# Two trunk layers on one core: hi and lo of an activation in one 512-column matmul, seven PSUM banks in one rotation, the queries' norm in the softmax

## The chip, the cores and the metric

One of the eight cores of a Trainium2 chip. The time is the device time of one execution in microseconds (us). PE is TensorE's matmul stream, PEld its weight loads, DVE VectorE, ACT ScalarE, POOL GpSimd, SP SyncE, which issues nearly all the DMAs.

## The reference, cut to what matters

256 tokens, 1024 channels, two layers, all float32. Only products with a weight matrix matter here:

```python
for l in range(DEPTH):                                  # DEPTH = 2
    u = rms_norm(h, norm_mix_g[l])
    p = u @ w_in[l]                                     # 1024 -> 10240: q, k, v, g_ret, c_in, gates
    y_a = (silu(g_ret) * o) @ w_ret_out                 # 2048 -> 1024, o: group-normed chunk retention
    y_b = c @ w_conv_out + b_conv_out                   # c: 31-tap conv, layer norm, silu
    h = h + (g_a * y_a + g_b * y_b) @ w_mix_out
    q = rms_norm(h, norm_xattn_g[l]) @ w_xq             # 4 heads of 256
    k, v = split(rms_norm(mem, norm_mem_g[l]) @ w_xkv)  # 256 memory tokens
    s = einsum("bshd,bmhd->bhsm", q, k) * 256 ** -0.5
    h = h + (softmax(s) @ v) @ w_xo
    val, gate = split(rms_norm(h, norm_ffn_g[l]) @ w_up)      # 1024 -> 2 * 2816
    h = h + (silu(causal_dwconv3(gate)) * val) @ w_down       # 2816 -> 1024
```

## The kernel before

Activations lie with the channel on the partitions: a block is 128 x 8 x 256 (8 channel tiles of 128, 256 tokens). Float32 precision is kept with two halves in a faster matmul format: `x = hi + lo`, and a product is the sum of three, `wh*uh + wh*ul + wl*uh`. So every weight and every activation has a hi tile and a lo tile.

`prepare` (lines 126 to 134) makes a weight *unit* (128 x 1024, eight channel tiles by 128 outputs): ACT copies the raw weights into `whi` (L131), DVE subtracts for `wlo` (L132). There are four places for units (UNITS), so unit u+4 can be made only when PE is done with unit u. `split` (L163, L164) does the same for an activation.

`feat` (L172 to L174) multiplies one unit with a block: per channel tile three matmuls of 256 columns, `wh` by `uh`, `wh` by `ul`, `wl` by `uh`, each with its own weight load, all summed into one half of a PSUM bank (a bank is 128 x 512). `both` (L274) is the same with two units taken in turn. `tok` (L185) is for products with the token on the partitions (v, g and the memory's v): there the weights move, 512 columns wide.

`run` goes through a list of steps, most of them two units wide: 40 for the in-projection (16 of them `tok`), then `w_ret_out`, `w_conv_out`, one chunk of the memory's keys (`mem_k`), `w_mix_out`, three more `mem_k`, the queries (`w_xq`) with attention between them, `w_xo`, `w_up`, `w_down`. The work between the steps (evacuation of banks, norms, retention, softmax) is recorded in program order, marked urgent in places, and put in order for each engine by a list scheduler that simulates the program.

PSUM has four banks in a rotation for these products (`mm`), three for attention (`att`) and one for the norms' sums (`nrm`). `residual` (L336) adds a bank to the residual stream `h`, squares it for the next norm, and, where a gain is given (`gained`), makes the hi and lo of `h * gain` at once (`early`), so that the next product can begin before its norm is known; its result is scaled afterwards (`scaled`). The queries don't do that: `normalise` builds normed hi and lo blocks under `mem_k` steps 1 to 3, and the softmax uses the constant 1/16.

Of the kernel before, what the change touches and what calls it, by code (L numbers as in the profile page):

```python
# [13 lines left out]
P = 128  # L14
# [30 lines left out]
BLOCKS = 10  # L45
# [6 lines left out]
def by_token(x):  # L52
    return x.rearrange("p k n -> p (k n)").rearrange("p (t d) -> p t d", t=2)

# [9 lines left out]
class Trunk:  # L64
# [19 lines left out]

    def block(self, dt=F32, tag="blk", bufs=BLOCKS):
        return self.bp.tile([P, KT, N], dt, name=self.nm(tag), tag=tag, bufs=bufs)
# [7 lines left out]
    def bank(self, tag="mm", bufs=4):  # L94
        return self.pp.tile([P, 2, N], F32, name=self.nm(tag), tag=tag, bufs=bufs)

# [78 lines left out]

    def tok(self, outs, ws, u, half):
# [13 lines left out]
    def flat_banks(self):  # L190
        return [self.bank().rearrange("p t n -> p (t n)") for _ in range(2)]
# [121 lines left out]
    @urgent  # L313
    def normalise(self, gname, layer, keep=False):
        r = self.spread(self.pending)
        if keep:
            self.rstd = self.small([N], "rstd", bufs=1)
            self.nc.scalar.activation(self.rstd, r, AF.Copy)
        return self.normed(self.h, r, gname, layer)

    def normed(self, h, rstd, gname, layer):
        nc = self.nc
        uh, ul = self.block(F32R), self.block(F32R)
        for j in range(KT // 2):
# [5 lines left out]
            self.split(u, uh[:, 2 * j:2 * j + 2, :], ul[:, 2 * j:2 * j + 2, :])  # L330
        return uh, ul
# [101 lines left out]

    def memory(self, layer):

        nc = self.nc
        m = self.block()
        nc.sync.dma_start(m, self.io["mem"])
# [6 lines left out]
        self.xk = self.block(F32R), self.block(F32R)  # L445
        self.xv = self.block(F32R), self.block(F32R)

    def mem_k(self, layer, c, midway=None):
        def fn(*w):
            ps, pr = self.bank(), slice(2 * c, 2 * c + 2)  # L450
            self.each(ps, w, self.mem, midway)
            self.split(ps, self.xk[0][:, pr, :], self.xk[1][:, pr, :])
        self.step(fn, *self.pair("w_xkv", layer, c))

    def mem_v(self, layer, c):

        def fn(*w):
            if c % 2 == 0:
# [9 lines left out]
    def mixer(self, layer):  # L468
# [5 lines left out]
        def alloc_conv():  # L474
            X["c"], X["cc"] = self.block(), self.block()

        def start():
            X["u"] = self.normalise("norm_mix_g", L, keep=True)
# [59 lines left out]
        def scores(h):  # L538
            ps = self.bank("att", 3).rearrange("p t n -> p (t n)")
# [9 lines left out]
        def attend(h):  # L549
            s, v = X["s", h], X["v", h]  # L550
            for n in range(2):
                ps = self.bank("att", 3).rearrange("p t n -> p (t n)")
# [18 lines left out]
        def gate(h):  # L571
            pt = [self.bank("att", 3) for _ in range(2)]
# [4 lines left out]
            hi, lo = X["y"]  # L577
            b, r = h // 2, (h % 2) * 4
            for f in range(4):
                src, gain = pt[f // 2][:, f % 2, :], self.par("ret_gn_g", L, 4 * h + f)  # L580
                yh, yl = hi[b][:, r + f, :], lo[b][:, r + f, :]
# [23 lines left out]
        def alloc_y():  # L605
            X["y"] = ([self.block(F32R), self.block(F32R)], [self.block(F32R), self.block(F32R)])
# [24 lines left out]
        def alloc_gates():  # L631
            X["gt"] = (self.block(), self.block())
# [16 lines left out]
        def alloc_m():  # L649
            X["m"] = self.block()  # L650
        self.step(alloc_m)
        for f in range(KT):
            def fn(*w, f=f):
                if f % 2 == 0:
                    X["ps"] = self.bank()
                hi, lo = X["y"]
                out = X["ps"][:, f % 2, :]
                for b in range(2):
                    self.feat(out, w[b], (hi[b], lo[b]), first=b == 0, last=b == 1)
                if f % 2:  # L660
                    pr = slice(f - 1, f + 1)
                    nc.vector.tensor_tensor(X["m"][:, pr, :], X["ps"], X["gt"][0][:, pr, :], op=ALU.mult)
            self.step(fn, *self.pair("w_ret_out", L, f))
            if f == MEM_AT:
# [11 lines left out]
        def conv_norm(self):  # L676
# [7 lines left out]
            r = self.spread(self.rsqrt(pair_sum(sq), LN_EPS))  # L684
            nc.vector.tensor_tensor(cc, cc, bc(r), op=ALU.mult)
            for k in range(KT):
                nc.scalar.activation(cc[:, k, :], cc[:, k, :], AF.Silu,
                                     scale=self.par("conv_ln_g", L, k),
                                     bias=self.par("conv_ln_b", L, k))
            X["z"] = self.block(F32R), self.block(F32R)  # L690
            self.split(cc, *X["z"])

        def alloc_mm():
            X["mm"] = self.block(F32R), self.block(F32R)
        self.step(alloc_mm)
        for j in range(4):
            def fn(*w, j=j):
                ps = self.bank()
                for f in range(2):
                    self.feat(ps[:, f, :], w[f], X["z"])  # L700
# [6 lines left out]
                m = X["m"][:, pr, :]  # L707
# [5 lines left out]
        self.begin()  # L713
# [300 lines left out]
```

## Time and profile before

| | |
|---|---|
| time, median of 3 runs | 1297.48 us (1297.29 to 1298.04) |
| profiled execution | 1297.52 us, its span 1295.7 us |
| PE busy | 1278.4 us, 99% of the span |
| PE's weight loads busy | 1225.2 us, 95% |
| DVE busy | 972.8 us, 75% |
| ACT busy | 857.7 us, 66% |
| TensorE's granted clock, mean | 0.997 of full speed |

The span runs from the first to the last instruction; the time of an execution has 1.8 us more. Busy time of PE says that matmuls were under way, not how fast they follow each other: a 256-column matmul is listed with some 283 ns, but several are in flight at once. How fast they follow is read from starts, or from a run of them and its count.

### The profile page before, as it was taken

Reading aid. Unit: us, or ns where it says so; the run is one execution under the profiler, and the core shown is the slowest. Engines: PE = TensorE matmul, PEld = TensorE weight load, DVE = VectorE, ACT = ScalarE, POOL = GpSimd, SP = SyncE. Lnnn points to the kernel's source line nnn. Section 1 sums busy time; section 2 is a strip of 40 time slices with the busy share of each in tenths; the row PEclk is TensorE's granted clock in tenths of the full one; section 3 lists DMA queues with packets and bytes.
Section 4 is the critical chain, followed back from the end, with each engine's and each line's share of the span. In section 5 each row is a group of like instructions: output and inputs, shape, how many; then the busy total and the mean of one; then the engine's idle time right before and its main releaser. Section 6 shows DMA issues by size and latency. Waiting matters only on the chain.

```text
span 1295.7 us, 23296 instructions
## 1 busy us (share of the span) xinstructions
PE 1278.4 (99%) x9632; PEld 1225.2 (95%) x9632; DVE 972.8 (75%) x1283; ACT 857.7 (66%) x1365; POOL 27.9 (2%) x31
## 2 busy tenths in 40 slices
PE   7999999999999999999999999999999999999997
PEld 7998888999999999999999888899999989999997
DVE  8989998767676688665677999985686766876653
ACT  6899999664445557664469899986454554666542
POOL 0000000000000000000000010000000000000000
PEclk9999999999999999999999999999999999999998
DMA  8554444555554445544555444444654544455450
GB/s 306 208 180 163 163 158 169 193 187 194 178 190 137 157 168 192 190 163 181 189 190 183 170 158 172 163 165 162 228 190 172 176 147 163 169 189 189 156 178 33
DMA packets 33082, 227.32 MB, mean 175 GB/s; under 512 B 3920, under 2 KB 4176, under 8 KB 6736
## 3 DMA queue, kind: packets, MB, share of 16 engines
q1 hardware_dynamic: 32688, 225.32, 49.4%
q8 instruction: 75, 1.23, 0.4%
q10 hardware_dynamic: 288, 0.52, 0.1%
q14 instruction: 31, 0.25, 0.1%
HBM read 224.78 MB, written 1.05 MB: 174 GB/s over the span
## 4 chain that ended last, share of the span: by engine, by line
PE 84%; issue 14%; DMA 0%; DVE 0%; ACT 0%; SPq 0%; POOLq 0%; POOL 0%; DVEq 0%
PE mm L172 20%; PE mm L173 20%; PE mm L174 20%; PE mm L185 17%; PE mm L274 3%; PE att L553 1%; PE att L745 1%; PE att L746 1%; PE att L744 1%; PE att L575 1%; PE att L542 1%; PE att L555 1%; PE nrm L211 0%; DMA raw<-in_w_in_dram 0%; PE nrm L203 0%
## 5 line engine op out<-in xcount | busy, mean ns | idle before, releaser
L172 PE MATMUL mm<-blk,whi 128*128 128x256 f32 x2624 | 745.4, 285 | 0.0
L173 PE MATMUL mm<-blk,whi 128*128 128x256 f32 x2624 | 742.3, 283 | 0.0
L174 PE MATMUL mm<-blk,wlo 128*128 128x256 f32 x2624 | 742.2, 283 | 0.0
L131 ACT ACTIVATE whi<-raw 128x1024 fp32r<-128x1024 f32 (+1 forms) x424 | 443.2, 1050 | 346.4 <-PE mm L173 270.7
L132 DVE TENSOR_TENSOR wlo<-raw,whi 128x1024 fp32r<-128x1024 f32 (+1 forms) x424 | 511.0, 1211 | 193.8 <-ACT whi L131 191.9
L172 PEld LDWEIGHTS mm<-blk,whi 128*128 128x128 f32 x2624 | 502.8, 192 | 2.6 <-issue 1.7
L173 PEld LDWEIGHTS mm<-blk,whi 128*128 128x128 f32 x2624 | 503.0, 192 | 2.3 <-issue 2.2
L174 PEld LDWEIGHTS mm<-blk,wlo 128*128 128x128 f32 x2624 | 502.9, 192 | 0.3 <-issue 0.2
L185 PE MATMUL mm<-whi,blk 128*128 128x512 f32 x640 | 201.9, 391 | 0.0
L499 ACT ACTIVATE prod<-blk,params 128x255 f32<-128x255 f32 (+14 forms) x480 | 197.2, 487 | 3.8 <-DVE blk L502 3.8
L502 DVE TENSOR_TENSOR blk<-blk,prod 128x1020 f32<-128x1020 f32 (+14 forms) x120 | 138.2, 1151 | 7.9 <-ACT prod L499 6.8
L185 PEld LDWEIGHTS mm<-whi,blk 128*128 128x128 f32 x640 | 119.6, 188 | 25.1 <-issue 1.2
L185 PE MATMUL mm<-wlo,blk 128*128 128x512 f32 x320 | 128.2, 401 | 0.0
L185 PEld LDWEIGHTS mm<-wlo,blk 128*128 128x128 f32 x320 | 60.1, 188 | 12.8 <-issue 0.7
L163 ACT ACTIVATE blk<-t 128x512 fp32r<-128x512 f32 (+1 forms) x71 | 42.5, 614 | 16.1 <-DVE t L261 12.4
L164 DVE TENSOR_TENSOR blk<-t,blk 128x512 fp32r<-128x512 f32 (+1 forms) x71 | 47.0, 676 | 2.6 <-ACT blk L163 2.6
L274 PE MATMUL mm<-blk,whi 128*128 128x256 f32 x192 | 39.7, 295 | 7.9 <-ACT whi L131 7.9
L274 PEld LDWEIGHTS mm<-blk,whi 128*128 128x128 f32 x192 | 32.5, 201 | 7.9 <-ACT whi L131 7.9
L848 DVE SCALAR_TENSOR_TENSOR t<-t,params,t 128x255 f32<-128x255 f32 (+1 forms) x88 | 38.2, 478 | 0.0
L336 DVE TENSOR_TENSOR h<-mm,h 128x512 f32<-128x512 f32 (+1 forms) x26 | 16.9, 650 | 20.9 <-PE mm L174 16.0
L274 PE MATMUL mm<-blk,wlo 128*128 128x256 f32 x96 | 28.3, 295 | 1.1 <-DVE wlo L132 1.1
L218 POOL TENSOR_TENSOR rs_r<-rs_m,mhalf 128x2 f32<-128x2 f32 x11 | 8.5, 777 | 888.5 <-DVE rs_m L217 888.5
(133 smaller groups left out, 742.4 us busy)
## 6 DMA issues: line engine op xcount, KB each, us to landing
raw<-in_w_in_dram SPq DMA_DIRECT2D x79, 1024.0 KB, 4.9
raw<-in_w_up_dram SPq DMA_DIRECT2D x44, 1024.0 KB, 4.9
raw<-in_w_ret_out_dram SPq DMA_DIRECT2D x16, 1024.0 KB, 4.9
raw<-in_w_xkv_dram SPq DMA_DIRECT2D x16, 1024.0 KB, 4.9
raw<-in_w_down_dram SPq DMA_DIRECT2D x16, 1024.0 KB, 5.0
raw<-in_w_conv_out_dram SPq DMA_DIRECT2D x8, 1024.0 KB, 5.8
raw<-in_w_mix_out_dram SPq DMA_DIRECT2D x8, 1024.0 KB, 4.8
raw<-in_w_xq_dram SPq DMA_DIRECT2D x8, 1024.0 KB, 4.8
```

The lines of the kernel that those rows point to most:

```text
L131: nc.scalar.activation(hi[:, :n], raw, AF.Copy)
L132: nc.vector.tensor_tensor(lo[:, :n], raw, hi[:, :n].bitcast(F32), op=ALU.subtract)
L163: self.nc.scalar.activation(hi, src, AF.Copy)
L164: self.nc.vector.tensor_tensor(lo, src, hi.bitcast(F32), op=ALU.subtract)
L172: self.nc.tensor.matmul(out, wh[:, k, :], uh[:, k0 + k, :], start=a, stop=False)
L173: self.nc.tensor.matmul(out, wh[:, k, :], ul[:, k0 + k, :], start=False, stop=False)
L174: self.nc.tensor.matmul(out, wl[:, k, :], uh[:, k0 + k, :], start=False, stop=b)
L185: mm = lambda a, b, p, q: self.nc.tensor.matmul(out, a[:, k, ts], b[:, j, :], start=p, stop=q)
L274: mm = lambda x, y, a, b: self.nc.tensor.matmul(out, x[:, k, :], y[:, k, :], start=a, stop=b, skip_group_check=True)
L499: nc.scalar.activation(t[:, i, :m], X["c"][:, k, :m], AF.Copy, scale=self.par("conv_dw_w", L, k * TAPS + TAPS - 1 - s))
L502: nc.vector.tensor_tensor(cc, cc, t[:, :, :m], op=ALU.add)
L848: nc.vector.scalar_tensor_tensor(g[:, f, s:], x[:, f, :N - s], wt(k, 2 - s), g[:, f, s:], op0=ALU.mult, op1=ALU.add)
```

## The change

1. Outside the in-projection (and the four chunks that run ahead of a norm), `feat` and `both` give way to `wide`: hi and lo of an activation lie side by side in one tile (`halved`, 128 x 8 x 2 x 256), and one matmul moves both, 512 columns, past `wh` into a whole PSUM bank; `wl` by `uh` follows with 256 columns into the bank's first half. The three partial products now lie in two halves of a bank.
2. The halves have to be added: `add_up` copies the second half to SBUF on ACT (L213) and adds the first on DVE (L214). `residual` adds all four halves to `h` on DVE (L380), with no copy.
3. The seven banks other than the norms' are one rotation; a product of two units takes two banks, not one.
4. The queries are made from `early`, hi and lo of `h * gain`, and the token's factor goes into the softmax's scale and maximum (`scale`, L778); the normed blocks for the queries are gone, two of the `mem_k` steps stand later, between the queries.
5. Smaller: `gained` takes hi by a scaled copy on ACT and lo by one DVE operation; blocks come in pairs; the memory's input lies in one of the four places for raw weights and is fetched two steps before its use; the conv norm's end goes in four pieces; in the FFN the gate's copy out of PSUM is gone.

```diff
+    def halved(self):
+        return Split(self.bp.tile([P, KT, 2, N], F32R, name=self.nm("blk"), tag="blk", bufs=BLOCKS))
...
-    def bank(self, tag="mm", bufs=4):
+    def bank(self, tag="mm", bufs=BANKS):
...
+    def wide(self, ps, w, u, first=True, last=True):
+        kt = w[0].shape[1]
+        for k in range(kt):
+            self.nc.tensor.matmul(ps, w[0][:, k, :], u.tile[:, k], start=first and k == 0, stop=False)
+            self.nc.tensor.matmul(ps[:, 0, :], w[1][:, k, :], u[0][:, k, :], start=False, stop=last and k == kt - 1)
+
+    def wides(self, w, u):
+        pair = self.banks()
+        for f in range(2):
+            self.wide(pair[f], w[f], u)
+        return pair
+
+    def add_up(self, pair):
+        t = self.temp()
+        for f, ps in enumerate(pair):
+            self.nc.scalar.activation(t[:, f, :], ps[:, 1, :], AF.Copy)
+            self.nc.vector.tensor_tensor(t[:, f, :], ps[:, 0, :], t[:, f, :], op=ALU.add)
+        return t
...
     def gained(self, k, n):
...
-            t, pr = self.temp(), slice(k, k + n)
-            for i in range(n):
-                nc.vector.tensor_scalar(t[:, i, :], self.h[:, k + i, :], self.par(*self.gain, k + i), None,
-                                        op0=ALU.mult)
-            self.split(t[:, :n, :], self.early[0][:, pr, :], self.early[1][:, pr, :])
+            for i in range(k, k + n):
+                hi, lo = (x[:, i, :] for x in self.early)
+                g = self.par(*self.gain, i)
+                nc.scalar.activation(hi, self.h[:, i, :], AF.Copy, scale=g)
+                nc.vector.scalar_tensor_tensor(lo, self.h[:, i, :], g, hi.bitcast(F32), op0=ALU.mult,
+                                               op1=ALU.subtract)
...
     @urgent
-    def residual(self, ps, k, n=2):
+    def residual(self, banks, k):
+        n = len(banks)
         h = self.h[:, k:k + n, :]
-        self.nc.vector.tensor_tensor(h, ps, h, op=ALU.add)
+        for f, ps in enumerate(banks):
+            for i in range(2):
+                self.nc.vector.tensor_tensor(h[:, f, :], ps[:, i, :], h[:, f, :], op=ALU.add)
         self.ssq_add(k, n, h)
         self.gained(k, n)
...
+    def fetch_memory(self):
+
+        raw = self.wp.tile([P, 2048], F32, name=self.nm("raw"), tag="raw", bufs=RAWS)
+        self.nc.sync.dma_start(raw, self.io["mem"])
...
-        def start():
-            X["u"] = self.normalise("norm_xattn_g", L)
-            X["o"] = self.block(F32R), self.block(F32R)
-        self.mem_k(L, 1, self.scale_of_h)
-        self.mem_k(L, 2, start)
-        self.mem_k(L, 3)
+        @urgent
+        def scale(self):
+
+            X["r"] = self.small([2], "xr", bufs=1)
+            nc.vector.tensor_scalar(X["r"], self.rms_scale()[1], 0.0625, None, op0=ALU.mult)
+        self.mem_k(L, 1)
...
-            nc.vector.tensor_scalar(nb, mx, -0.0625, None, op0=ALU.mult)
+            nc.vector.scalar_tensor_tensor(nb, mx, -1.0, X["r"], op0=ALU.mult, op1=ALU.mult)
...
-                nc.scalar.activation(p[:, t, :], ps[:, t, :], AF.Exp, scale=0.0625,
+                nc.scalar.activation(p[:, t, :], ps[:, t, :], AF.Exp, scale=X["r"][:, t:t + 1],
```

Three places show how the instructions move. First PE, at the end of one unit and the start of the next in `w_up` of layer 0 (L172 to L174 are `feat`'s three matmuls, L200 and L201 `wide`'s two; behind the arrow what is written and read, then partitions by columns). Before:

```order
L173 MATMUL mm_817_5464<-blk_787_5312,whi_805_5391 128x256
L174 MATMUL mm_817_5464<-blk_786_5311,wlo_806_5392 128x256
L172 MATMUL mm_817_5464<-blk_786_5311,whi_807_5395 128x256
L173 MATMUL mm_817_5464<-blk_787_5312,whi_807_5395 128x256
L173 MATMUL mm_825_5533<-blk_787_5312,whi_813_5456 128x256
L174 MATMUL mm_817_5464<-blk_786_5311,wlo_808_5396 128x256
```

Of the change:

```order
L200 MATMUL mm_881_5452<-blk_800_4973,whi_868_5393 128x512
L201 MATMUL mm_881_5452<-blk_800_4973,wlo_869_5394 128x256
L200 MATMUL mm_889_5508<-blk_800_4973,whi_876_5443 128x512
L201 MATMUL mm_889_5508<-blk_800_4973,wlo_877_5444 128x256
L200 MATMUL mm_889_5508<-blk_800_4973,whi_876_5443 128x512
```

Three matmuls of 256 columns have become one of 512 and one of 256, and each unit fills a bank of its own.

Second DVE, at the residual adds of `w_mix_out` in layer 0 (L132 and L151 are the weights' lo, L336 and L380 the adds to `h`, L231 and L272 the norm's sum of squares, L304 the lo of `early`). Before:

```order
L132 TENSOR_TENSOR wlo_578_3866<-raw_576_3863,whi_577_3865 128x1024
L336 TENSOR_TENSOR h_77<-mm_574_3811,h_77 128x512
L132 TENSOR_TENSOR wlo_580_3870<-raw_576_3863,whi_579_3869 128x1024
L132 TENSOR_TENSOR wlo_586_3930<-raw_584_3927,whi_585_3929 128x1024
L336 TENSOR_TENSOR h_77<-mm_581_3873,h_77 128x512
L132 TENSOR_TENSOR wlo_588_3934<-raw_584_3927,whi_587_3933 128x1024
L231 TENSOR_TENSOR t2_583_3925<-t2_575_3861,t2_582_3923 128x512
```

Of the change:

```order
L380 TENSOR_TENSOR h_77<-mm_584_3704,h_77 128x256
L151 TENSOR_TENSOR wlo_590_3753<-raw_588_3750,whi_589_3752 128x1024
L380 TENSOR_TENSOR h_77<-mm_585_3705,h_77 128x256
L151 TENSOR_TENSOR wlo_592_3757<-raw_588_3750,whi_591_3756 128x1024
L380 TENSOR_TENSOR h_77<-mm_593_3760,h_77 128x256
L304 SCALAR_TENSOR_TENSOR blk_575_3649<-h_77,params_76,blk_575_3649 128x256
L151 TENSOR_TENSOR wlo_599_3809<-raw_597_3806,whi_598_3808 128x1024
L304 SCALAR_TENSOR_TENSOR blk_575_3649<-h_77,params_76,blk_575_3649 128x256
L272 TENSOR_TENSOR t2_587_3744<-t2_578_3688,t2_586_3742 128x512
L304 SCALAR_TENSOR_TENSOR blk_575_3649<-h_77,params_76,blk_575_3649 128x256
```

Between the weights' subtractions stand now single 256-column adds of four banks and the lo of `early`, where one 512-column add stood.

Third PE, inside `w_mix_out` of layer 0, where the last pieces of its input come late. Before, two banks are worked on in turn, the first two steps' first units:

```order
L174 MATMUL mm_574_3811<-blk_538_3488,wlo_565_3743 128x256
L172 MATMUL mm_574_3811<-blk_538_3488,whi_564_3742 128x256
L172 MATMUL mm_581_3873<-blk_538_3488,whi_570_3803 128x256
L173 MATMUL mm_581_3873<-blk_539_3489,whi_570_3803 128x256
L174 MATMUL mm_581_3873<-blk_538_3488,wlo_571_3804 128x256
```

Of the change, four banks (576, 577, 584, 585) and with them all four units are worked on in turn, and the next two units follow at once:

```order
L200 MATMUL mm_584_3704<-blk_530_3377,whi_571_3641 128x512
L201 MATMUL mm_584_3704<-blk_530_3377,wlo_572_3642 128x256
L200 MATMUL mm_585_3705<-blk_530_3377,whi_573_3645 128x512
L201 MATMUL mm_585_3705<-blk_530_3377,wlo_574_3646 128x256
L200 MATMUL mm_585_3705<-blk_530_3377,whi_573_3645 128x512
L201 MATMUL mm_585_3705<-blk_530_3377,wlo_574_3646 128x256
L200 MATMUL mm_593_3760<-blk_530_3377,whi_580_3696 128x512
L200 MATMUL mm_594_3761<-blk_530_3377,whi_582_3700 128x512
L201 MATMUL mm_593_3760<-blk_530_3377,wlo_581_3697 128x256
```

So the four places for units come free within a short stretch there, and their successors are wanted right behind it.

## Rows read from the trace of the kernel before

**Rows 1.** The page: busy time, clock in 40 slices, chain, one kind of DMA issue.

```profile
span 1295.7 us, 23296 instructions
PE 1278.4 (99%) x9632; PEld 1225.2 (95%) x9632; DVE 972.8 (75%) x1283; ACT 857.7 (66%) x1365; POOL 27.9 (2%) x31
...
PEclk9999999999999999999999999999999999999998
...
PE 84%; issue 14%; DMA 0%; DVE 0%; ACT 0%; SPq 0%; POOLq 0%; POOL 0%; DVEq 0%
...
raw<-in_w_ret_out_dram SPq DMA_DIRECT2D x16, 1024.0 KB, 4.9
```

**Rows 2.** The waits: who waited for whom, us in total, times, longest.

```profile
PE mm L274 <- ACT whi L131: 7.9, 1, 7.9
PE mm L274 <- DVE wlo L132: 1.1, 2, 0.7
PE nrm L211 <- POOL rs_r L218: 1.1, 1, 1.1
PE nrm L203 <- ACT t L224: 0.6, 1, 0.6
...
ACT whi L131 <- PE mm L173: 270.7, 204, 2.3
```

**Rows 3.** The chain in order of time: start us, us, what, count.

```profile
107.71 14.08 PE mm L185 x62
...
303.56 0.44 PE nrm L211 x4
...
648.40 5.04 PE mm L274 x42
...
744.07 10.91 PE mm L185 x48
```

**Rows 4.** Windows: us, then busy us (count) of PE, PEld, DVE, ACT, POOL, clock, DMA.

```profile
97.00:224.00 127.00, 127.00 (x733) 108.94 (x733) 118.49 (x159) 119.72 (x239) 10.27 (x8) 1.00 0.47 159
...
336.00:359.00 23.00, 23.00 (x194) 23.00 (x193) 14.37 (x15) 10.48 (x13) 0.00 (x0) 1.00 0.53 183
...
467.00:586.00 119.00, 119.00 (x995) 119.00 (x994) 90.17 (x124) 76.38 (x102) 0.00 (x0) 1.00 0.52 182
737.00:861.00 124.00, 124.00 (x715) 106.61 (x714) 116.23 (x158) 116.76 (x234) 8.83 (x8) 1.00 0.47 163
```

**Rows 5.** Timeline of DVE in `w_conv_out`, layer 0: start us, us.

```profile
316.12 1.21 DVE L132 TENSOR_TENSOR wlo<-raw,whi 128x1024 fp32r<-128x1024 f32 x1
317.95 0.88 DVE L704 SCALAR_TENSOR_TENSOR t<-mm,params,blk 128x256 f32<-128x256 f32 x2 [0.62 <-PE mm L174]
318.75 0.68 DVE L164 TENSOR_TENSOR blk<-blk,blk 128x512 fp32r<-128x512 f32 x1
319.35 1.22 DVE L132 TENSOR_TENSOR wlo<-raw,whi 128x1024 fp32r<-128x1024 f32 x1
320.48 0.68 DVE L708 TENSOR_TENSOR blk<-blk,t 128x512 f32<-128x512 f32 x1
```

**Rows 6.** Groups by shape: DVE in 586 to 658 us, ACT in 220 to 240.

```profile
L132 DVE TENSOR_TENSOR wlo<-raw,whi 128x1024 fp32r<-128x1024 f32 x20 | 24.4, 1225 | 18.4 <-ACT whi L131 18.4
...
L336 DVE TENSOR_TENSOR h<-mm,h 128x256 f32<-128x256 f32 x2 | 0.8, 422 | 0.4 <-PE mm L174 0.4
...
L131 ACT ACTIVATE whi<-raw 128x1024 fp32r<-128x1024 f32 x7 | 7.3, 1062 | 0.3 <-PE mm L173 0.3
L638 ACT ACTIVATE blk<-mm,params 128x256 f32<-128x256 f32 x8 | 3.3, 472 | 0.0
```

**Rows 7.** Timeline at the end: the last adds, sums and the output.

```profile
1284.86 0.42 DVE L336 TENSOR_TENSOR h<-mm,h 128x256 f32<-128x256 f32 x1 [7.49 <-PE mm L174]
1285.32 0.42 ACT L224 ACTIVATE t<-h 128x256 f32<-128x256 f32 x1 [7.10 <-DVE h L336]
...
1285.79 1.05 PE L203 MATMUL nrm<-ones,t 128*128 128x1 f32 x8 [0.63 <-ACT t L224]
```

More of the change, by code (lines that the diff above doesn't have):

```diff
@@ L44 @@
 UNITS = 4
-BLOCKS = 10
+BLOCKS = 5
+BANKS = 7
 TEMPS = 8
@@ L190, in flat_banks @@
     def flat_banks(self):
-        return [self.bank().rearrange("p t n -> p (t n)") for _ in range(2)]
+        return [x.rearrange("p t n -> p (t n)") for x in self.banks()]
     def halves(self, x):
@@ L444, in memory, with mem_k @@
         self.mem = self.normed(m, r, "norm_mem_g", layer)
-        self.xk = self.block(F32R), self.block(F32R)
-        self.xv = self.block(F32R), self.block(F32R)
-    def mem_k(self, layer, c, midway=None):
+        self.xk = self.halved()
+    def mem_k(self, layer, c):
         def fn(*w):
-            ps, pr = self.bank(), slice(2 * c, 2 * c + 2)
-            self.each(ps, w, self.mem, midway)
-            self.split(ps, self.xk[0][:, pr, :], self.xk[1][:, pr, :])
+            pr = slice(2 * c, 2 * c + 2)
+            pair = self.wides(w, self.mem)
+            self.split(self.add_up(pair), self.xk[0][:, pr, :], self.xk[1][:, pr, :])
         self.step(fn, *self.pair("w_xkv", layer, c))
@@ L457, in fn @@
         def fn(*w):
+            if c == 0:
+                t = self.blocks(F32R)
+                self.xv = t[:, 0], t[:, 1]
             if c % 2 == 0:
@@ L571, in gate @@
         def gate(h):
-            pt = [self.bank("att", 3) for _ in range(2)]
+            pt = [self.bank() for _ in range(2)]
             for n in range(2):
@@ L654, in fn @@
                 if f % 2 == 0:
-                    X["ps"] = self.bank()
-                hi, lo = X["y"]
-                out = X["ps"][:, f % 2, :]
+                    X["ps"] = self.banks()
                 for b in range(2):
-                    self.feat(out, w[b], (hi[b], lo[b]), first=b == 0, last=b == 1)
+                    self.wide(X["ps"][f % 2], w[b], X["y"][b], first=b == 0, last=b == 1)
                 if f % 2:
-                    pr = slice(f - 1, f + 1)
-                    nc.vector.tensor_tensor(X["m"][:, pr, :], X["ps"], X["gt"][0][:, pr, :], op=ALU.mult)
+                    m = X["gt"][0][:, f - 1:f + 1, :]
+                    nc.vector.tensor_tensor(m, self.add_up(X["ps"]), m, op=ALU.mult)
             self.step(fn, *self.pair("w_ret_out", L, f))
+            if f == MEM_AT - 2:
+                self.step(self.fetch_memory)
             if f == MEM_AT:
@@ L697, in fn @@
             def fn(*w, j=j):
-                ps = self.bank()
-                for f in range(2):
-                    self.feat(ps[:, f, :], w[f], X["z"])
+                ps = self.add_up(self.wides(w, X["z"]))
                 t = self.temp()
@@ L788, in cross @@
         q_step(0)
+        self.step(lambda: scale(self))
+        self.mem_k(L, 2)
         q_step(1)
         do(scores, 0)
+        self.mem_k(L, 3)
         q_step(2)
@@ L811, in fn @@
             def fn(*w, j=j):
-                ps = self.bank()
-                (self.each if j else self.both)(ps, w, X["o"])
-                self.residual(ps, 2 * j)
+                self.residual(self.wides(w, X["o"]), 2 * j)
             self.step(fn, *self.pair("w_xo", L, j))
@@ L872, in fn @@
             def fn(*w, f=f):
-                if f % 2 == 0 or f == KT - 1:
-                    X["ps"] = self.bank()
-                at = f % 2 if f < KT - 2 else 0
+                if f % 2 == 0:
+                    X["ps"] = self.banks()
                 for b in range(3):
-                    self.feat(X["ps"][:, at, :], w[b], X["a"][b], first=b == 0, last=b == 2)
+                    self.wide(X["ps"][f % 2], w[b], X["a"][b], first=b == 0, last=b == 2)
                 if f >= KT - 2:
-                    self.residual(X["ps"][:, 0:1, :], f, 1)
+                    self.residual([X["ps"][f % 2]], f)
                 elif f % 2:
```

114 lines of the change are left out of this document (57 added, 57 removed).

## The prediction, made before the changed kernel ran

> **What bounds the kernel now.** I read the page first: PE is busy for 99% of the span, and the chain that ended last is 84% PE, its other 14% "issue", time in which nothing was waited for [rows 1]. Busy time alone proves little, so the waits come next. PE waits four times in the whole execution, 10.7 us in all, 9 of them at the very start and 1.7 in the last norm [rows 2]; in between it never stands. ACT, on the other side, waits 270.7 us for PE to give back a place for weights [rows 2]: the engines that feed PE run ahead of it. So the time is PE's instruction stream, at the pace at which matmuls follow each other.
>
> That pace I take from runs of one shape in the chain: 42 matmuls of 256 columns in 5.04 us are 120.0 ns each; 62 of 512 columns in 14.08 us and 48 in 10.91 are 227.1 and 227.3 ns each [rows 3]. A stage of `w_up` alone agrees, 995 in 119 us, 119.6 each; some records are missing in such counts, so I take 120.0 [rows 4]. The granted clock is 1.00 there, the 2.4 GHz level [rows 4]; at that level the columns alone are 106.7 and 213.3 ns (256 and 512 by 2.4, worked out), so either shape pays some 13 ns on top, once per instruction and not per column.
>
> **The change, part by part.** *Matmuls.* Three of 256 columns (360.0 ns) become one of 512 and one of 256 (227.1 + 120.0 = 347.1 ns): 12.9 ns saved for each channel tile of a unit. Converted tiles per layer: `w_ret_out` 16 units by 8 = 128; `w_conv_out`, `w_mix_out`, `mem_k`, `w_xq`, `w_xo` 8 units by 8 = 64 each, 320; `w_up` without the chunks run ahead, 36 units by 8 = 288; `w_down` 8 by 22 = 176. Together 912, in two layers 1824. 1824 by 12.9 ns = 23.5 us less. The columns stay the same; what goes is one fixed share per tile.
>
> No row shows the two shapes taking turns. Above, the pair can cost the 360 of before; below, if the narrow matmul's fixed share also vanished behind the wide one, 347.1 - 13.3 = 333.8 ns, 47.8 us saved. I take 347.1, since both uniform runs load new weights for each matmul just as the pair does. The Trainium skill (TensorE: Matmul & The Clock Gate, section Back-to-back issue gap) gives a gap of N/2.4 + 2.5 ns when warm, a fixed share of 2.5 ns. By that rule 1824 instructions fewer would be 4.6 us, and the rows, with 13 to 14 ns, do not follow it.
>
> *Norm of the queries.* Two `spread` calls go, 0.44 us of PE each [rows 3]: 0.9 us less. The sum and root stay, and must be ready for the first softmax; in program order `w_xq`'s first step, a `mem_k` step and a second query step stand between, 16.7 us of PE at 5.55 a step (16 by 347.1), so the scale is not what is late, and the weights' lo queued behind it on DVE is not held.
>
> *The halves' sum.* 136 copies on ACT and 136 adds on DVE. Not in the trace with this use; nearest rows: 0.472 us for a 256-column ACT read of PSUM, 0.422 for such an add on DVE [rows 6]. `residual` has 96 adds of 0.42 (40 us) for 22 of 0.68 and 4 of 0.42 (17 us). ACT gets 64 us, DVE 57 + 23 = 80, less some 14 for the normed blocks of the queries (16 operations of 0.4 to 0.5, 8 of 0.68). DVE would be at 973 + 66 of about 1275, 81%. All of it lies beside PE, if it lies there stage by stage. Back to back (start to start) DVE needs 1.13 us for a weight's lo, 0.60 for 512 columns, 0.40 for 256 [rows 5]. A step of `w_conv_out`: 2 by 1.13 + 2 by 0.40 (sum) + 2 by 0.40 + 2 by 0.60 = 5.06. One of `w_mix_out` or `w_xo`: 2.26 + 4 by 0.40 + 0.60 + 2 by 0.40 = 5.26. PE needs 5.55. A pair of `w_up` steps: 8.92 of 11.1. Before, `w_mix_out` had DVE busy 14.4 of 23 us [rows 4]. So DVE still fits everywhere, at 91% and 95% in three stages. A unit can be made while PE works on three others, 8.3 us, and needs 1.06 + 1.22 [rows 5, 6]: DVE may fall 6 us behind before PE stands.
>
> *Places where the order is tight.* In `w_mix_out` (and likewise in `w_xo`) the order uses up all four units together. From a unit's end to its successor's lo PE has six pairs and two wide matmuls, 2.5 us; DVE first does three of the 256-column adds, the third when the second bank is done 0.7 us later, and then makes lo: 0.7 + 0.40 + 1.22, about 2.4 with the hand-over. Bounds 0 and 0.5 us, four times: 0 to 2; with other such spots I take 1.5 us lost.
>
> *End and start.* After the last matmul comes one more add, 0.42 at most [rows 7]: 0.4 us more. At the start ACT makes hi of x first and DVE two operations fewer; the first weights still arrive later than that, so 0.
>
> *Moved at no cost.* The memory's input takes one of four raw places and goes out on SP ahead of the last `w_ret_out` weights. A raw fetch lands in 4.9 us [rows 1]; the three places that are left cover three steps, 16.6 us. If that cover were gone, one fetch would be late once per layer, at most 4.9 us. The two `mem_k` steps moved take their fetches and unit preparations along, one for one with the query steps that they change places with.
>
> Sum, from the profiled 1297.5 us (the median of the runs, 1297.48, is the same): - 23.5 - 0.9 + 1.5 + 0.4 = 1275.0 us.
>
> **Rivals.** *DVE paces the residual stages.* For it: 95% there, and each bank now needs two operations after a hand-over. DVE stood 0.62 us for PE ahead of such an evacuation [rows 5]. With one such gap per step, 5.88 us against 5.55 in 16 steps (`w_mix_out`, `w_xo`) and 5.68 in 8 (`w_conv_out`): 6 us; with two, one for each bank, 6.50 and 6.30: 21 us. Against it: 6 us of lag are free in each of six stages. Time 1281 to 1296, most likely 1284.
>
> *The pair does not follow the uniform pace.* If the change of shape costs what the missing instruction saved, the pair stays near 360: half of it 1287, none 1298.5. For it: the shapes never took turns so far. Against: three separate runs give one fixed share. (By the Trainium skill's rule cited above, 4.6 us saved, the time would be 1294; it lies in this case and has some 0.01 of its chance, as the rows contradict it.)
>
> *One rotation holds PE up in the retention: slower.* In its two stretches (251 us, eight heads) DVE is busy 93% and ACT 94% [rows 4], and the banks of the attention, freed only after a long chain over POOL, now stand in the products' way. It decides from 22.5 / 8 = 2.8 us per head on; at 4 us per head 32 us, 1307. Against it: a head takes 31.4 us and eleven banks, so seven are 20 us of lead; before, six product banks by four were 21 us and five attention banks by three 19. The lead hardly changes.
>
> **How the numbers follow.** Forecast 0.77 (its own range 1270 to 1281), DVE 0.11, pair 0.05, rotation 0.06, better than 1270 0.01. The range 1270 to 1288 takes the forecast and the cheaper half of the DVE case, 0.83; the pair's lower bound (333.8 ns, 1251) has the last 0.01. Within 0.2% (2.6 us, about what a measurement of this kernel can tell from no change) lies the pair at nothing saved, 0.04; slower is the rotation, 0.06; the rest, 0.90, is faster.
>
> **What would show it.** Right: runs of `wide` in the chain at 347 ns a pair; PE's waits still under some 5 us between start and end; DVE near 81%; ACT still waiting for PE. Wrong: pairs near 360 ns; PE waits on `wlo` or `h` in `w_mix_out` and `w_xo`; PE waits in the retention for an attention bank.

## The result, and the profile after

The changed kernel takes 1282.37 us (median of 4 runs, 1281.44 to 1282.83), the kernel before 1297.41 in the same session: ratio 0.9882, 95% interval 0.9865 to 0.9899. It is 15.0 us faster; 22.5 us had been forecast. The time lies in the range given, 1270 to 1288, but 1.4 us above the forecast case's own, 1270 to 1281. The profiled execution took 1282.83 us, its span 1280.9.

The page of the changed kernel, first the lines that answer to [rows 1]:

```profile
span 1280.9 us, 20050 instructions
...
PE 1261.6 (98%) x7800; PEld 1125.2 (88%) x7800; DVE 1024.1 (80%) x1478; ACT 891.6 (70%) x1513; POOL 29.8 (2%) x31
...
PEclk9999999999999999999999999999999999999998
...
PE 95%; DVE 2%; ACT 2%; DMA 1%; issue 0%; SPq 0%; POOLq 0%; DVEq 0%
...
L200 PE MATMUL mm<-blk,whi 128*128 128x512 f32 x1824 | 636.4, 395 | 0.0
...
L201 PE MATMUL mm<-blk,wlo 128*128 128x256 f32 x1824 | 505.4, 280 | 0.0
...
L380 DVE TENSOR_TENSOR h<-mm,h 128x256 f32<-128x256 f32 x96 | 38.6, 419 | 32.9 <-PE mm L201 32.2
L214 DVE TENSOR_TENSOR t<-mm,t 128x256 f32<-128x256 f32 x136 | 55.0, 416 | 0.0
L213 ACT ACTIVATE t<-mm 128x256 f32<-128x256 f32 x136 | 47.8, 366 | 0.0
```

PE lists 1832 instructions fewer: 1824 from the merged matmuls, 8 from the two spreads (each is listed as four). DVE is 80% busy, ACT 70%. The new work is there as priced: 96 and 136 adds of 0.42 us on DVE, 136 copies on ACT, these at 0.37 us rather than the 0.47 taken from [rows 6]. The chain is PE in 95%; "issue" has gone from it, but neither share says how fast PE's matmuls follow each other.

The waits of the changed kernel (who for whom, us in total, times, longest), against [rows 2]:

```profile
ACT whi L150 <- PE mm L200: 191.1, 149, 5.2
...
PE mm L316 <- ACT whi L150: 8.7, 1, 8.7
...
PE nrm L244 <- ACT t L265: 1.1, 1, 1.1
PE nrm L252 <- POOL rs_r L259: 1.1, 1, 1.1
PE mm L193 <- DVE wlo L151: 0.8, 1, 0.8
PE mm L316 <- DVE wlo L151: 0.8, 2, 0.5
PE mm L226 <- DVE wlo L151: 0.4, 1, 0.4
```

Nothing large is new: 0.8 and 0.4 us for a unit's lo part in the first layer's retention (L193, L226), 0.5 more at the end (1.1 for 0.6). ACT still waits for PE. So the missing 7.5 us are mostly not in waits that this view lists, and the pace of the pairs had to be looked at.

Windows of the first layer's `w_up` (without the chunks run ahead) and `w_down`, from the first matmul of each to the first of the next stage. First the changed kernel, then the kernel before (columns as in [rows 4]):

```profile
480.60:580.55 99.95, 99.95 (x578) 87.41 (x577) 87.22 (x138) 68.56 (x112) 0.00 (x0) 1.00 0.56 194
580.55:642.54 61.99, 61.99 (x355) 53.87 (x353) 39.41 (x52) 30.06 (x38) 0.00 (x0) 1.00 0.50 186
```

```profile
481.20:584.88 103.68, 103.68 (x867) 103.68 (x865) 75.28 (x101) 66.14 (x87) 0.00 (x0) 1.00 0.53 188
584.88:648.24 63.36, 63.36 (x531) 63.36 (x529) 36.66 (x44) 28.23 (x33) 0.00 (x0) 1.00 0.50 182
```

`w_up` has 288 tiles here and takes 3.73 us less than before; 288 by 12.9 ns is 3.72, so there the pair costs the 347.1 ns of the forecast. `w_down` has 176 tiles and takes 1.37 us less where 2.27 were forecast: 352 ns a pair, at the same clock, with DVE less busy (39 of 62 us against 87 of 100). Over the whole execution, gaps with a stand left out, the mean is 349.2 ns, 233.0 from a wide start to the next start and 116.2 from a narrow one. The starts show two paces, each kept for long stretches (ns, wide + narrow, worked out from the starts):

```
w_up,   from 500 us:  231+112 233+117 231+113 232+118 231+112 233+117 ...   (346.5 a pair)
w_down, from 598 us:  233+117 241+120 236+113 233+117 241+120 236+113 ...   (353.3 a pair)
```

The second sort of loss is small and lies in the attention. The timeline of the changed kernel behind the last `turn` of the first layer (start us, us):

```profile
430.34 1.38 DVE L183 TENSOR_TENSOR blk<-mm,blk 128x512 fp32r<-128x512 f32 x2 [0.35 <-ACT blk L182]
...
430.74 0.28 PE L790 MATMUL mm<-t,blk 128*128 128x256 f32 x1
...
431.08 0.19 PEld L791 LDWEIGHTS mm<-t,blk 128*128 128x128 f32 x1 [0.26 <-DVE blk L183]
...
431.42 0.28 PE L790 MATMUL mm<-t,blk 128*128 128x256 f32 x1
...
431.76 0.19 PEld L791 LDWEIGHTS mm<-t,blk 128*128 128x128 f32 x1 [0.27 <-DVE blk L183]
```

The weight load of L791 stands for a lo part that DVE has just begun: 0.34 us from L790's start to L791's where 0.12 is normal, and 0.1 more behind it. With a third such place at 415 us that is 0.9 us per layer. In the kernel before the same matmuls follow each other at 0.12, with single gaps of 0.2. The wait is listed under PEld and not under PE, which is why the list above does not have it.

### The profile page after: what moved, and what is told of

Its sections match the earlier page's. It is cut to its first block, busy times and chain, and to the rows that moved or that the text cites. A ratio compares the mean times of both kernels' runs of the same rounds, so it can differ in the third digit from the quotient of the medians.

```text
span 1280.9 us, 20050 instructions
## 1 busy us (share of the span) xinstructions
PE 1261.6 (98%) x7800; PEld 1125.2 (88%) x7800; DVE 1024.1 (80%) x1478; ACT 891.6 (70%) x1513; POOL 29.8 (2%) x31
## 4 chain that ended last, share of the span: by engine, by line
PE 95%; DVE 2%; ACT 2%; DMA 1%; issue 0%; SPq 0%; POOLq 0%; DVEq 0%
PE mm L200 33%; PE mm L201 17%; PE mm L226 16%; PE mm L191 7%; PE mm L193 7%; PE mm L192 7%; PE mm L316 2%; PE mm L605 1%; PE mm L791 1%; DVE wlo L151 1%; PE mm L789 1%; ACT prod L551 1%; PE mm L790 1%; PE mm L627 1%; PE mm L594 1%; PE mm L607 1%
## 5 line engine op out<-in xcount | busy, mean ns | idle before, releaser
L200 PE MATMUL mm<-blk,whi 128*128 128x512 f32 x1824 | 636.4, 395 | 0.0
L151 DVE TENSOR_TENSOR wlo<-raw,whi 128x1024 fp32r<-128x1024 f32 (+1 forms) x424 | 511.0, 1210 | 152.0 <-ACT whi L150 148.2
L201 PE MATMUL mm<-blk,wlo 128*128 128x256 f32 x1824 | 505.4, 280 | 0.0
L200 PEld LDWEIGHTS mm<-blk,whi 128*128 128x128 f32 x1824 | 340.4, 188 | 76.6
L201 PEld LDWEIGHTS mm<-blk,wlo 128*128 128x128 f32 x1824 | 343.7, 188 | 3.4 <-DVE wlo L151 1.0
L191 PE MATMUL mm<-blk,whi 128*128 128x256 f32 x832 | 239.2, 288 | 0.0
L193 PE MATMUL mm<-blk,wlo 128*128 128x256 f32 x832 | 235.1, 283 | 0.8 <-DVE wlo L151 0.8
L192 PE MATMUL mm<-blk,whi 128*128 128x256 f32 x832 | 235.3, 283 | 0.0
L226 PE MATMUL mm<-whi,blk 128*128 128x512 f32 x640 | 203.8, 393 | 0.0
L192 PEld LDWEIGHTS mm<-blk,whi 128*128 128x128 f32 x832 | 159.4, 192 | 2.0 <-issue 1.9
L191 PEld LDWEIGHTS mm<-blk,whi 128*128 128x128 f32 x832 | 159.3, 192 | 2.0 <-issue 1.7
L193 PEld LDWEIGHTS mm<-blk,wlo 128*128 128x128 f32 x832 | 159.2, 192 | 1.2 <-DVE wlo L151 1.2
L226 PEld LDWEIGHTS mm<-whi,blk 128*128 128x128 f32 x640 | 119.6, 188 | 24.6 <-issue 1.0
L226 PE MATMUL mm<-wlo,blk 128*128 128x512 f32 x320 | 127.5, 399 | 0.4 <-DVE wlo L151 0.4
L226 PEld LDWEIGHTS mm<-wlo,blk 128*128 128x128 f32 x320 | 60.2, 188 | 13.5 <-issue 1.0
L380 DVE TENSOR_TENSOR h<-mm,h 128x256 f32<-128x256 f32 x96 | 38.6, 419 | 32.9 <-PE mm L201 32.2
L214 DVE TENSOR_TENSOR t<-mm,t 128x256 f32<-128x256 f32 x136 | 55.0, 416 | 0.0
L213 ACT ACTIVATE t<-mm 128x256 f32<-128x256 f32 x136 | 47.8, 366 | 0.0
L888 DVE SCALAR_TENSOR_TENSOR t<-t,params,t 128x255 f32<-128x255 f32 (+1 forms) x88 | 40.8, 477 | 0.6
```

The lines of the kernel that those rows point to most:

```text
L151: nc.vector.tensor_tensor(lo[:, :n], raw, hi[:, :n].bitcast(F32), op=ALU.subtract)
L191: self.nc.tensor.matmul(out, wh[:, k, :], uh[:, k0 + k, :], start=a, stop=False)
L192: self.nc.tensor.matmul(out, wh[:, k, :], ul[:, k0 + k, :], start=False, stop=False)
L193: self.nc.tensor.matmul(out, wl[:, k, :], uh[:, k0 + k, :], start=False, stop=b)
L200: self.nc.tensor.matmul(ps, w[0][:, k, :], u.tile[:, k], start=first and k == 0, stop=False)
L201: self.nc.tensor.matmul(ps[:, 0, :], w[1][:, k, :], u[0][:, k, :], start=False, stop=last and k == kt - 1)
```

## Experiments

Theory: PE still sets the time; what is missing is the price of the pair (349.2 for 347.1 ns, 4 us) and some 3 us of small waits. Rivals: DVE, with its added sums, sets the pace somewhere; or the parts "of no cost" (rotation, norm) do more than was thought.

**e1_grouped: wide ones first, narrow ones after**

```diff
         for k in range(kt):
             matmul(ps, w[0][:, k, :], u.tile[:, k], ...)
+        for k in range(kt):
             matmul(ps[:, 0, :], w[1][:, k, :], u[0][:, k, :], ...)
```

> Edit: within a unit all eight 512-column matmuls go first, then the eight of 256 columns. The trace of the changed kernel shows its pairs at two paces, each held for a whole stretch: 346.8 ns (1105 pairs) and 353.2 ns (673 pairs), the latter through all of w_down, for instance. Theory A (the turn-taking of the two shapes makes the second pace): in runs of one shape each matmul goes at 227.1 and 120.0 ns, 347.1 a pair everywhere, so 4 us less than the changed kernel: 1278.4 us, perhaps 1 us less again, since a unit's lo part is now needed 1.8 us later. Theory B (the stages pay for something else, such as evacuations that read the banks beside PE): the second pace stays in the same stages, 1282.4 us, within 1 us.

Measured: 1282.11 us, ratio 0.9879 (0.9864 to 0.9894), no different from the changed kernel. Theory A's 4 us did not come. Nor does B hold: the two paces are gone. The same two stages in e1_grouped:

```profile
480.04:580.52 100.48, 100.48 (x578) 88.45 (x577) 86.80 (x138) 69.21 (x113) 0.00 (x0) 1.00 0.55 194
580.52:641.99 61.47, 61.47 (x355) 54.07 (x354) 38.53 (x51) 29.59 (x39) 0.00 (x0) 1.00 0.52 191
```

Both now cost 349 ns a pair (100.48 by 288; 61.47 by 176): `w_up` became slower, `w_down` faster. One unit's starts show where it goes:

```
wide 233 236 228 232 231 227 226 227, narrow 113 119 120 120 120 120 120 120   (ns to the next start)
```

The first wide ones behind a run of narrow ones are up to 9 ns above 227.1, and the narrow ones give back only 8: 15 ns for each change to wide and back, 2 ns per pair. So grouped, a change of shape costs something; taking turns costs nothing at one of its paces and 6 ns at the other.

The traces of the runs below, which also take turns, settle theory B: the pace does not belong to the stage (means of pairs without a stand, worked out from the starts). In the changed kernel `w_up` goes at 347.0 ns a pair and `w_down` at 352.2, in both layers. In e12_six `w_down` goes at 346.7 in both layers; in e4_rotback `w_up` of the second layer goes at 353.4 and the `w_down` behind it at 347.7; in e6_banks52 the first `w_up` goes at 353.0, in e7_double the second at 352.5. What selects the pace is not shown.

**e2_three: the wide matmul as two narrow ones**

```diff
-            matmul(ps, w[0][:, k, :], u.tile[:, k], ...)
+            for i in range(2):
+                matmul(ps[:, i, :], w[0][:, k, :], u[i][:, k, :], ...)
             matmul(ps[:, 0, :], w[1][:, k, :], u[0][:, k, :], ...)
```

> Edit: the changed kernel with its 512-column matmul issued as two of 256 columns with the same weights into the two halves of the same bank; the sum of the halves, the one rotation of banks and the queries' norm stay. It measures what everything but the merged matmul costs. Theory A (pairs at 349.3 ns on average against 360.0, 10.7 ns by 1824 tiles = 19.5 us, and 4.5 us lost elsewhere): 1282.4 + 19.5 = 1301.9 us, and the uniform narrow matmuls at 120.0 ns in the trace. Theory B (the prediction's 12.9 ns hold and the loss elsewhere is larger, 8.4 us): 1305.9 us. Theory C (the halves' sum holds PE up by itself, and the longer tiles hide it): under 1300 us.

Measured: 1301.51 us, ratio 1.0027 (1.0016 to 1.0038). Theory A. The merged matmul is worth 1301.51 - 1282.37 = 19.1 us, 10.5 ns per tile, and all the rest of the change costs some 4 us (2.1 to 4.9 by the interval). Its `w_up` and `w_down` are those of before to 0.01 us:

```profile
484.18:587.87 103.69, 103.69 (x866) 103.69 (x865) 88.57 (x140) 68.64 (x112) 0.00 (x0) 1.00 0.54 186
587.87:651.23 63.36, 63.36 (x530) 63.36 (x529) 39.43 (x52) 30.28 (x38) 0.00 (x0) 1.00 0.51 184
```

DVE is busy 13 us longer in this `w_up` than before, and PE does not notice. The 4 us are elsewhere: the same three waits per layer in the attention, the same waits for a lo part in the first retention (1.0 and 0.6 us from start to start), the end.

**e3_normback and e5_normmid: the queries' norm ahead of their projection again**

```diff
-        self.begin(("norm_xattn_g", L))
+        self.begin()
...
+        def start():
+            X["u"] = self.normalise("norm_xattn_g", L)
+        self.mem_k(L, 1, self.scale_of_h)      # e5: midway in the step, as before
+        self.mem_k(L, 2, start)
+        self.mem_k(L, 3)
...
-    AF.Exp, scale=X["r"][:, t:t + 1]
+    AF.Exp, scale=0.0625
```

(e3 has the two calls as steps of their own, ahead of the `mem_k` steps.)

> Edit: the changed kernel with the queries' norm ahead of their projection again, in a block of its own, with the order of steps that goes with it; the wide matmuls stay. Theory A (the norm in the softmax is worth the two spreads and no more): 0.9 us slower than the changed kernel, 1283.3 us. Theory B (the waits of the attention's matmuls on the turned weights, some 0.2 to 0.5 us at a time near 415 and 430 us and again in layer 2, come from the new order of steps): not slower, 1281 to 1282.4 us, and these waits are gone.

> Edit: the changed kernel with the queries' norm ahead of their projection, placed just as before the change: the sum in the middle of the second mem_k step, the spread in the middle of the third, 1.5 steps (8.3 us) of PE work ahead of the first product that needs the block. The run e3_normback put it elsewhere and PE stood 5.4 us per layer for the last half of that block. Theory A (only its place made that wait): two spreads at 0.44 us, some 0.9 to 1.5 us slower than the changed kernel, 1283.3 to 1284 us. Theory B (with the halves' sums DVE has no room for the block in 8.3 us: eight products at 0.40, four lo at 0.68, three lo of weights at 1.22, three sums at 0.40, about 10.8 us): PE stands 2.5 us or more per layer, and after it goes at half the clock for some us as in e3_normback: 1288 us or more.

Measured: 1297.41 us (0.9988 to 1.0007) and 1297.31 us (0.9987 to 1.0006), 15 us slower than the changed kernel and no faster than before. Neither theory of e3 had that; for e5 it is theory B, larger than expected. e5_normmid's wait, and the windows around it in the first layer:

```profile
PE mm L200 <- DVE blk L183: 10.8, 2, 5.4
```

```profile
375.30:381.00 5.70, 0.38 (x3) 0.06 (x1) 5.70 (x14) 4.66 (x9) 0.00 (x0) 0.95 0.16 57
381.00:386.00 5.00, 4.92 (x15) 4.28 (x16) 2.94 (x5) 0.00 (x0) 0.00 (x0) 0.50 0.56 206
386.00:388.50 2.50, 2.50 (x12) 2.15 (x12) 0.00 (x0) 0.00 (x0) 0.00 (x0) 0.75 0.00 0
388.50:392.00 3.50, 3.50 (x23) 3.06 (x22) 1.56 (x2) 2.25 (x3) 0.00 (x0) 1.00 0.00 0
```

PE stands 5.4 us for the normed block while DVE works without a pause (5.70 of 5.70). Then the granted clock reads 0.50, the 1.2 GHz level, for 5 us: pairs go at 640 ns, some 2.2 us lost, and 0.4 more until it is at 1.00. Two layers by (5.4 + 2.6) is 16.0 us, and the two spreads add 0.9; the two profiled executions differ by 16.0 us (1298.82 and 1282.83).

**e9_normmemk and e10_normmix: which sums made the block late**

Both are e5_normmid with one stage back in three narrow matmuls and one bank, without a sum of halves: `mem_k` in e9, `w_mix_out` in e10.

```diff
-            pair = self.wides(w, self.mem, midway)
-            self.split(self.add_up(pair), ...)
+            ps = self.bank()
+            self.each(ps, w, self.mem, midway)
+            self.split(ps, ...)
```

> Edit: as e5_normmid (the queries' norm ahead of their projection), and mem_k in its old form, three 256-column matmuls a tile into one bank, no sum of halves there. In e5_normmid PE stood 5.4 us per layer for the normed block. Theory A (the sums of mem_k's halves, which DVE and ACT run in the stretch that should cover the norm, make the block late): the wait falls below 1.5 us per layer and the clock stays up; 128 tiles lose 10.7 ns (1.4 us), two spreads 0.9: 1285 to 1288 us. Theory B (the block is late because the stage before, w_mix_out with its four adds a step, ends its sum of squares later; in e5_normmid the sum came to PE 3.5 us later than before the change): the wait stays above 3 us per layer, 1294 us or more.

> Edit: as e5_normmid, and w_mix_out in its old form (three 256-column matmuls a tile into one bank, one add of 512 columns a step); mem_k stays wide. The other half of e9_normmemk. Theory A (mem_k's halves' sums are the cause): PE still stands 3 us or more per layer for the block, 1294 us or more. Theory B (w_mix_out's end is the cause): the wait is below 1.5 us per layer, 1285 to 1288 us. If both halves of the pair shorten the wait in part, it is the sum of the two on DVE.

Measured: 1288.69 us (ratio 0.9931, 0.9913 to 0.9949) and 1290.97 us (0.9949, 0.9933 to 0.9964). The wait of e9, and the windows of the stand and of what follows it:

```profile
PE mm L200 <- DVE blk L183: 3.4, 2, 1.7
```

```profile
375.40:377.30 1.90, 0.27 (x3) 0.07 (x1) 1.90 (x4) 1.65 (x3) 0.00 (x0) 1.00 0.25 104
377.30:380.00 2.70, 2.60 (x14) 2.31 (x15) 2.70 (x4) 0.42 (x1) 0.00 (x0) 1.00 0.02 6
```

The same of e10:

```profile
PE mm L200 <- DVE blk L183: 4.6, 2, 2.3
```

```profile
376.80:379.30 2.50, 0.29 (x2) 0.00 (x0) 2.50 (x6) 2.50 (x5) 0.00 (x0) 1.00 0.29 121
379.30:383.00 3.70, 3.59 (x20) 3.19 (x21) 3.70 (x6) 0.56 (x2) 0.00 (x0) 1.00 0.02 4
```

Either one takes 3 us or more off each stand, and with the shorter stand the clock stays at 1.00 in the profiled execution (in e10 the slowest of the four, 1292.34 us, has a mean clock of 0.995 against 0.998, so there it may have fallen). So it is not one stage. For `mem_k`, e5_normmid's DVE shows how: between the norm's eight products (L371) and the lo parts of the block (L183) stand three sums of halves (L216), a weight's lo (L151) and one more sum.

```profile
374.65 3.21 DVE L371 SCALAR_TENSOR_TENSOR t<-h,params,nrm 128x256 f32<-128x256 f32 x8
377.78 1.08 DVE L216 TENSOR_TENSOR t<-mm,t 128x256 f32<-128x256 f32 x3
378.78 1.22 DVE L151 TENSOR_TENSOR wlo<-raw,whi 128x1024 fp32r<-128x1024 f32 x1
379.91 0.42 DVE L216 TENSOR_TENSOR t<-mm,t 128x256 f32<-128x256 f32 x1
380.25 1.89 DVE L183 TENSOR_TENSOR blk<-t,blk 128x512 fp32r<-128x512 f32 x3
```

That the sums of `w_mix_out` make the norm begin late is argued, not shown: the norm's sum comes to PE 1.4 us earlier in e10 (366.3 for 367.7 us), but 1.3 earlier in e9 too. In e9 theory A's limit of 1.5 us and in e10 theory B's were missed; that both halves shorten the stand is the third case named in e10's expectation.

**e11_beforesoft: the norm in the softmax alone**

The edit is part 4 of the change, on the kernel before.

> Edit: the kernel before with only the queries' norm moved into the softmax (and the order of steps that goes with it); narrow matmuls, both rotations of banks and the blocks of before stay. It closes the square of wide matmuls and norm: neither 1297.5, wide alone 1297.3 (e5_normmid), both 1282.4. Theory A (the norm was covered before, so moving it saves two spreads): 0.9 us faster than before, 1296.6 us. Theory B (it cost more than its spreads there too): 1293 us or less.

Measured: 1296.72 us, ratio 0.9993 (0.9983 to 1.0002): 1.0 us faster by the medians, with no change at all inside the interval. Theory A, as far as it can be seen. The square is closed: norm alone 1.0, wide matmuls and the rest with the norm ahead 0.5 (e5_normmid), both 15.0.

**e4_rotback, e6_banks52, e12_six: the banks**

```diff
-    def bank(self, tag="mm", bufs=BANKS):
+    def bank(self, tag="mm", bufs=4):          # e6: 5
...
-            ps = self.bank()                   # in the attention
+            ps = self.bank("att", 3)           # e6: 2
```

e12 keeps one rotation, with `BANKS = 6`.

> Edit: four banks for products and three for the attention, as before the change, in place of one rotation of seven; all else as changed. Theory A (the lead of the banks hardly matters): within 1 us of 1282.4. Theory B (the products of two banks a step need more than four banks): slower, since a step's pair of banks must be freed by the step before the last, 3 us or more, with waits of PE for a bank in w_up and w_mix_out. Theory C (the one rotation holds PE up in the retention): faster by 1 us or more.

> Edit: as e4_rotback (two rotations of banks), but five for products and two for the attention instead of four and three. In e4_rotback PE stood 4.7 us per layer for the scaling of the chunks that are run ahead, which hold three banks. Theory A (the first w_up step needs two banks, and three of four are held): with five it has two at once, the wait is gone, and the time is 1282.4 us plus what two banks cost the attention, 1282 to 1286 us. Theory B (the scaling itself is late, however many banks there are): the waits of 4.7 us per layer stay, about 1297 us.

> Edit: the changed kernel with six banks in its one rotation instead of seven. With five product banks (e6_banks52) PE stood 3.6 us per layer at the second w_up step, with four (e4_rotback) 4.7 us at the first. Theory A (the chunks run ahead hold three banks, and the two w_up steps that follow need two each, seven in all): with six the second step still lacks one, PE stands there 2 to 3.6 us per layer and goes at half the clock after it, 1287 to 1292 us. Theory B (the attention's small share of banks made those waits, not the count): 1282.4 us within 1 us.

Measured: 1297.62 us (0.9988 to 1.0007), 1291.86 us (0.9939 to 0.9969) and 1283.63 us (0.9875 to 0.9911). The waits for banks, in that order; in e4 at the first step of `w_up`, in e6 and e12 at the second:

```profile
PE mm L200 <- DVE t L332: 9.4, 2, 4.7
```

```profile
PE mm L200 <- DVE t L214: 7.1, 2, 3.6
```

```profile
PE mm L200 <- DVE t L214: 1.1, 2, 0.5
```

The chunks run ahead hold three banks until their norm is known. Of four product banks one is then left, and the first step of `w_up` needs two: e4's theory B by its size, though it stands in `w_up` alone. With five the first step goes and the second stands: e6's theory A was right on the cause and wrong that one more bank would do. Six leave 0.5 us per layer, so e12's theory A overrated it; seven leave none. The time of e12 says less than its wait: in its profiled execution `w_down` goes at the faster pace in both layers, which is worth 1.9 us. As in e5_normmid each long stand is paid twice, here in e4_rotback (a stand, then the clock at 0.50):

```profile
485.40:490.30 4.90, 0.29 (x2) 0.00 (x0) 3.73 (x5) 4.11 (x6) 0.00 (x0) 0.89 0.70 236
490.30:495.80 5.50, 5.43 (x17) 4.68 (x18) 4.06 (x9) 2.38 (x6) 0.00 (x0) 0.50 0.40 167
```

**e7_double: one more DVE operation for each bank**

```diff
             vector.tensor_tensor(t[:, f, :], ps[:, 0, :], t[:, f, :], op=ALU.add)
+            vector.tensor_scalar(t[:, f, :], t[:, f, :], 1.0, None, op0=ALU.mult)
```

(and the same on `h` in `residual`)

> Edit: the changed kernel with one more DVE operation per bank behind each sum of halves and each residual (times 1.0, 256 columns, in place), 184 in all at some 0.33 us, 60 us of DVE, which would be 84% busy. Theory A (outside the retention DVE has slack, and its lag is free up to 6 us per stage): less than 2 us slower, under 1284.5 us, no new wait of PE above 1 us. Theory B (DVE already sets the pace in w_mix_out, w_xo and w_conv_out, and the part of the gain that is missing is lost there): 0.66 us more per step in 24 steps, up to 16 us slower, 1290 us or more, with PE waits on lo parts of weights.

Measured: 1287.34 us, ratio 0.9920 (0.9905 to 0.9934): 5.0 us slower than the changed kernel, between the theories. The page's busy line:

```profile
PE 1264.5 (98%) x7800; PEld 1125.1 (88%) x7800; DVE 1057.1 (82%) x1662; ACT 892.5 (69%) x1513; POOL 28.8 (2%) x31
```

33 us more of DVE, and 5 us more of time. The starts show gaps of 0.2 to 0.35 us in `w_mix_out`, in `w_xo`, in the chunks ahead and early in `w_up`; with the 0.1 us that most have behind them they are 3.5 us in both layers, where the changed kernel has 0.4. Another 1.6 us is the second layer's `w_up` at the slower pace of the pairs, 352.5 ns for 347.0; that DVE brought this about is not shown. DVE has slack, but the tight places have none.

**e8_inwide: the in-projection too**

```diff
-                ps = self.bank()
-                for f in range(2):
-                    self.feat(ps[:, f, :], w[f], X["u"])
-                evac(ps)
+                evac(self.add_up(self.wides(w, X["u"])))
```

> Edit: the in-projection's channel steps take the wide matmul and the sum of halves too (16 tiles a step; the chunks run ahead and the token steps stay). 20 steps a layer, 640 tiles in two layers: PE would gain 640 by 10.7 ns = 6.8 us. DVE and ACT get 80 more operations each of 0.42 and 0.37 us: 33.6 and 29.6 us, in the retention, where they were 93 and 94% busy. Theory A (they have no room there): the retention is paced by them, some 10 us or more slower than the changed kernel, 1290 us or more, with PE waits on wlo. Theory B (their lag fits): 1276 us.

Measured: 1316.85 us, ratio 1.0150 (1.0135 to 1.0165), 34 us slower than the changed kernel. Theory A, but with other waits: not for weights, but for the rotated keys at the end of a DVE chain,

```profile
PE mm L591 <- DVE k L584: 27.9, 8, 5.6
```

eight times, up to 5.6 us, and as above behind seven of these stands the granted clock reads 0.50, with pairs at 640 ns. The in-projection is better left as it was.

## Why the prediction was right, and what it had wrong

**What bounds the kernel.** Right: PE's stream, 98% busy, no new wait above 1 us, and the gain comes out of the merged matmuls (e2_three).

**Matmuls, 12.9 ns per tile.** The mechanism was right, the size not: 10.5 ns by e2_three, 10.8 by the starts. In `w_up` the pair does cost 347.1; in `w_down` it goes mostly at the slower pace, 353.3, and grouped it costs 349. 1824 tiles give 19.1 us and not 23.5: 4.4 of the missing 7.5 us. The step that was too bold is to take 347.1 "since both uniform runs load new weights for each matmul just as the pair does": no row showed the shapes taking turns, and the turns have a second pace that neither uniform run has. Since its share changes from kernel to kernel, 10.5 ns is what this one got, not a constant of the pair. The rival "pair does not follow the uniform pace" was right in kind, at a sixth of the 12.9 ns. By the rule of the Trainium skill (TensorE: Matmul & The Clock Gate, section Back-to-back issue gap) 4.6 us would have been saved; 19.1 were. But that section gives the 2.5 ns for a single matmul by itself, and says that in a stream of weight loads and matmuls both set the spacing, so the rule did not apply here. The fixed share in this kernel is the larger one that [rows 3] show.

**Norm of the queries, 0.9 us.** As a term of the sum it was right (1.0 us in e11_beforesoft). But it was priced on the old cover, while with the sums of halves on DVE that cover is gone: without this part the rest gains nothing (e5_normmid, 1297.31). The sentence "DVE still fits everywhere" holds only because the normed blocks left DVE.

**The halves' sum.** DVE at 80% for 81 forecast, ACT 70%. In time the forecast was too high, 51 us more on DVE for 66 and 34 on ACT for 64; the cheaper copies (0.37 for 0.47 us) are 14 of ACT's 30. `w_up` and `w_down` hide it fully (e2_three). The six free microseconds of lag are not there at each place: e7_double.

**Tight places, 1.5 us.** The sum was too small and the places were others. In `w_mix_out` and `w_xo` the loss is 0.1 us each per layer (start to start, 0.4 in all). The attention, not considered, loses 0.9 per layer; the first layer's retention 1.6. The end: 0.5 for 0.4. That is 4.3, less 0.9 for the spreads 3.4, against the 4 us of e2_three (forecast 1.0); 0.6 is not located.

**Start, 0.** 8.7 us to the first weights instead of 7.9. The first weights land later there. e2_three has the same code at the start and 7.9, so the edit does not force it; but e8_inwide has 8.3 and the other nine runs with this start 8.6 to 8.8, while e11_beforesoft, with the start of before, has 8.0. Whether the edit brings it about stays open. By these profiles e2_three has 0.8 us less at the start than the changed kernel, so the 19.1 us may be that much too low; 10.8 ns by 1824 is 19.7.

**Rivals.** DVE as the pace: not in the changed kernel, but close by (e5, e7, e8). One rotation as a hindrance: the reverse, it is worth 15 us (e4_rotback), because two-bank steps meet three held banks.

## What to carry to other kernels

Price each part of a change on the kernel that has the other parts, too: here a norm worth 1 us and a bank rotation priced at nothing are each worth 15 us, since each removes a wait that the two-bank steps or their sums of halves would bring. When a stage's evacuation moves to DVE, recount the cover of every chain that runs on DVE behind it, not only the busy share of the stage. And where two shapes will take turns that never did, keep a share of the saving in doubt.

## What the runs showed of the hardware

The same instruction mix of turns between 512 and 256 columns ran at 346.8 ns a pair (1105 pairs) or 353.2 (673) in the changed kernel, each pace kept for long stretches. The same stage took either pace from one kernel to the next (`w_down` 352.2 in the changed kernel, 346.7 in e12_six); what selects it stays open. Grouped by eight, both stages came to 349. The uniform stages show no second pace: those of e2_three take what they took before, 120.0 ns a matmul.

In the profiled executions, after stands of 5.4, 4.7 and 3.6 us (e5, e4, e6) and seven of 2.8 to 5.6 us in e8 the granted clock read 0.50, the 1.2 GHz level, and pairs took 640 ns; after 2.3 and 1.7 us (e10, e9) it read 1.00. The Trainium skill (TensorE: Matmul & The Clock Gate, section HAM oscillation — how this bites in real kernels) has it that stretches without matmuls bring the half clock; these runs agree, and here the half clock adds some 2.6 us to a stand of 5.4.
